# Twelve prepare steps per pair in FFN1, the mixer's running sums in two tiles, head 0's q and k loaded in the last unit

## The chip, the cores and the metric

The kernel runs on one core of a Trainium2 chip. Its time is device microseconds of one execution; the median of several executions is compared. The trace is of one further execution, taken by the hardware profiler. The engines are TensorE (PE, with its weight load PEld), VectorE (DVE), ScalarE (ACT), GpSimd (POOL) and SyncE (SP, which here only issues transfers). All are programmed in order, each with its own queue.

## The reference

One encoder block on x of 1024 tokens by 1024 features, all in float32:

```python
x = layer_norm(a*x + 0.5*swiglu(x, ffn1...))          # FFN1, hidden width 4096
z = x @ w_in                                          # 1024 x 2568: q, k, v, lx, lg, forget logits
fox = forgetting_attention(q, k, v, fg)               # 8 heads of 64, causal, with a forget bias
rec = rg_lru(conv(lx)); lru = gelu(lg) * rec          # a gated linear recurrence, 512 channels
x = layer_norm(a*x + concat(fox, lru) @ w_out)
x = layer_norm(a*x + 0.5*swiglu(x, ffn2...))          # FFN2
```

with a = 2^0.25. `swiglu(x) = (silu(x @ w_gate) * (x @ w_up)) @ w_down`.

## The kernel before

**Numbers and products.** Each float32 operand is split in two parts in a reduced format, `hi` (a cast on ACT) and `lo` (a subtraction on DVE), and a product takes three matmuls (`mm3`, lines 165 to 167). Large products use a seven-product scheme on 2 x 2 blocks (after Strassen and Winograd): the operands are sums and differences of blocks, named "11", "t1", "t2", "s1" and so on, and running sums of products in PSUM give the results.

**FFN1's gate_up.** `gate_up` (line 367 on) goes through 16 pairs of 128-column weight blocks. A pair has two matrices, gate and up. For each matrix, `weights` loads 1 MB (line 400) into one of two "raw" tiles and makes seven operands of two tiles each (`parts`, lines 385 and 386; `less`, line 391) out of the 15 "ws" tiles of a pool. Then come the products, in steps named `one`, (`four` of the matrix before, as `pending`), `two`, `six`, `five`, `seven`, `three`. Some copy the result out of PSUM on ACT (`one` line 690, `six` 696, `five` 700, `four` 709), others add on DVE (`two` 693, `seven` 703, `three` 706). The end of a pair (`finish`, lines 729 to 739) makes the operands of the next stage on DVE and stores them to `h_d` from POOL's queue.

**Prepare steps.** The later stages need kept operands of their weights: those of the mixer's w_in and of the first pair of FFN2. They depend on inputs only, and the generator `prepare` makes them one by one while FFN1 runs. An operand takes a load of 128 KB into one of four "aux" tiles (SP, line 276), sometimes a difference (`less`, line 287), a cast (ACT, line 282) and a subtraction (DVE, line 283) into one "ws" tile of the same pool as the weights, and a store (POOL, line 284) to `wv_d`, `wq_d` or `pre_d`. The generator stops once after its first four loads, and once after each operand: 16 operands for v, 8 units x 2 halves x 7 for the rest of the mixer, 2 matrices x 2 halves x 7 for FFN2, 156 in all. In the loop over pairs 1 to 15, `next(steps)` is called behind three of the six steps of each matrix. What is left afterwards is run in a loop behind `gate_up`:

```python
        for _ in steps:
            pass
```

**FFN1's down_ffn.** It loads the kept operands of `h_d` and blocks of w_down (line 107; the first block goes where operand s3 of gate_up was), splits them (`parts`, lines 810 and 813) and takes seven products.

**The mixer.** `mixer_in` computes z in eight `unit`s of seven products. Units alternate: 128 LRU channels, then 128 columns of q and of k. A unit takes one PSUM tile of two banks, `total` and `z`, from a pool of two (`psS`), and an "a" tile for product "12". In order: "11" into total, copy (1150); "12"; "s2" onto total, copy (1157); "s1" into z, copy (1160); "s3" onto total, add (1163); "s4" onto z, add (1166); "22" onto total. `then[7]` reads total out at the end: LRU units by a copy (line 1201), q/k units by `store`, an activation (1214) and a subtraction (1215) into tiles that go to `q_d` or `k_d` from POOL's queue. Weights come as `wq` (line 1130), three loads ahead. In the last unit the four rows of w_out that belong to the LRU half are loaded (1257) and split (157 and 158).

**Attention.** `attention` takes 64 units (head, block of 128 rows). Scores (1312, 1313), sum with the forget bias and row maximum on DVE (1318), exponential on ACT (1319), scaling on POOL (1322), transposes (1333), values (1354). `load(h)` brings q, k (two parts), cum and v of a head (lines 1291 to 1296). Between units, "pieces" of the output product of the LRU half fill TensorE (`down_tile`, added to the rows of x1 by line 233); `open_row` loads those rows (1396), and `out_w` the other half of w_out (1273).

**What sets the order.** A planner orders the instructions of each engine by the order of the program and by a model of the costs, and inserts the waits. It may move an instruction ahead of its place in the program when it is ready sooner. `issue_after(ins)` forbids what follows on the engine of `ins` to be queued ahead of it; it waits for nothing. Tiles of one tag share the pool's buffers: a tile waits until the last use of the one that had its buffer.

Of the kernel before, what the change touches and what calls it, by code (L numbers as in the profile page):

```python
# [61 lines left out]
class Block:  # L62
# [202 lines left out]
    def prepare(self, jobs, wsp, ap):  # L265
# [104 lines left out]
    def gate_up(self, wg, wu, h_d, rows, bank, tp, wsp, raws=None, later=None, aside=None, ready=None, steps=None):  # L370
# [301 lines left out]
        class Matrix:  # L672
# [22 lines left out]
            def six(m):  # L695
                nc.scalar.copy(m.u, m.product("t2", "s2", m.sum))  # L696

            def five(m):
                m.z = m.product("t1", "s1")
                nc.scalar.copy(m.s5, m.z)  # L700
# [18 lines left out]
        for pair in range(FF // P // 2):  # L719
# [331 lines left out]

    def mixer_in(self, w_out, vw, vp, wp):
# [7 lines left out]
        with self.tc.tile_pool(name="lru_t", bufs=1, reuse_waits="tile") as tp, \  # L1060
# [80 lines left out]
            def unit(c0, c1, c3, then):  # L1141
# [5 lines left out]
                s = self.s_tile()  # L1147
                total, z = s[:, 0, :], s[:, 1, :]
# [9 lines left out]
                done(3)  # L1158
                product(z, "s1")
# [92 lines left out]

            def load_rows():
                for f in range(4):
                    w_rows.append(vp.tile([P, D], F32, tag=f"w{(f + 1) % 4}", name=self.nm("wout")))
                    with self.tc.issue_after(self.row_load.ins):
                        self.row_load = nc.sync.dma_start(w_rows[f], w_out[FOX + f * P:FOX + (f + 1) * P, :])

            def split_row():
                self.lru_w.append(tuple(t[:, 0, :] for t in self.split_ws(w_rows[len(self.lru_w)].rearrange("p (k c) -> p k c", k=1), 1)))  # L1260
# [16 lines left out]
    def attention(self, w_out, mixp, ln, x1_d, normed):  # L1277
# [4 lines left out]
        with self.pool("att_p", 3) as pp, self.pool("att_t", 1) as tp, self.pool("att_pt", 6) as ptp, self.pool("att_qk", 2, side="right") as qkp:  # L1282

            def load(h):
                vt = qkp.tile([P, NT, P], F32R, tag="v", name=self.nm("v"))
                cum = qkp.tile([P, T], F32, tag="cum", name=self.nm("cum"))
                q, kh, kl = (qkp.tile([P, T], F32R, tag=t, name=self.nm(t)) for t in ("q", "kh", "kl"))
                mine = slice(64 * (h % 2), 64 * (h % 2) + 64)
                for j in range(2):
                    rows = slice(64 * j, 64 * j + 64)  # L1290
                    nc.sync.dma_start(f32(q[rows]), self.q_d[h // 2, j, mine, :])
                    nc.sync.dma_start(f32(kh[rows]), self.k_d[h // 2, 0, mine, :])
                    nc.sync.dma_start(f32(kl[rows]), self.k_d[h // 2, 1, mine, :])
                row = self.cum_d[h:h + 1, :]
                nc.sync.dma_start(cum, bass.AP(tensor=row.tensor, offset=row.offset, ap=[[0, P], [1, T]]))
                v_load = nc.sync.dma_start(f32(vt), self.v_d[h].rearrange("(j p) d -> p j d", p=P))
                if h == 0:
                    self.row_load = v_load
                return q, kh, kl, vt, cum
# [106 lines left out]

            piece()
            piece()
# [8 lines left out]
            for n in range(len(units) + AHEAD + 1):  # L1417
# [42 lines left out]
def kernel(  # L1460
# [49 lines left out]
    with blk.psum():  # L1510
        left = ExitStack()
        blk.wsp = left.enter_context(blk.pool("mx_ws", 8))
        with blk.pool("dn_v", side="right") as vp, blk.pool("dn_w", side="right") as wp:
            first = []

            def hooks(norm):
# [6 lines left out]
                def v_weights(g):  # L1523
# [16 lines left out]
                      lambda i: nc.gpsimd.dma_start(x2_d[(i + 4) % NT * P:((i + 4) % NT + 1) * P, :], blk.acc[i]))  # L1540
        rows = blk.acc[4:] + blk.acc[:4]
# [66 lines left out]
```

## Time and profile before

| | |
|---|---|
| runs (us) | 2427.19, 2432.87, 2427.22 |
| median | 2427.22 |
| profiled execution | 2425.57, span 2423.9 |
| TensorE busy | 2290.4 of the span |
| DVE, ACT, POOL busy | 1720.0, 1064.9, 311.1 |
| mean granted clock of TensorE | 0.977 |

The profiled execution is one of its own; its time lies near the median. FFN1's gate_up runs to 641 us, its down_ffn from 726 to about 1030, the mixer's units from 1087 to 1272, attention from 1288 to about 1505, FFN2's gate_up to 2110 and its down_ffn to the end.

In the views quoted below, a wait reads "engine line waited for: total us, times, longest"; a row of the timeline "start, duration, engine, line, operation, output<-inputs", with the idle time before it and what ended it in brackets; a group of instructions "busy us, mean ns of one | idle before and what ended it"; a stretch "from:to, length, busy us (and count) of PE, PEld, DVE, ACT and POOL, granted clock, share of DMA, GB/s"; a transfer "output<-input, queue, count, KB each, us from issue to landing".

### The profile page before, as it was taken

How to read it: one execution, taken by the hardware profiler on the slowest of the kernel's cores; microseconds unless marked ns; L12 is line 12 of the kernel's file. 1: busy time of each engine (PE TensorE's matmuls, PEld its weight loads, DVE VectorE, ACT ScalarE, POOL GpSimd, SP SyncE). 2: the span in 40 equal slices, each digit the busy share in tenths (PEclk: the TensorE clock that was granted, in tenths of full speed). 3: DMA queues.
4: the chain of work that ended last, by engine and by line, in shares of the span. 5: the costliest groups of instructions: out<-in, count | busy, mean ns of one | idle time of the engine just before them, and what ended most of it. 6: DMA issues, size and time to landing. Idle time of an engine off the chain costs nothing.

```text
span 2423.9 us, 29536 instructions
## 1 busy us (share of the span) xinstructions
PE 2290.4 (94%) x10609; PEld 1897.6 (78%) x10609; DVE 1720.0 (71%) x2745; ACT 1064.9 (44%) x1767; POOL 311.1 (13%) x505
## 2 busy tenths in 40 slices
PE   9999999999509999999997999999999999999998
PEld 7888887888408888897776878888888888888887
DVE  8777766676447778786765889766665656567886
ACT  5444443444334434444554675533433333344342
POOL 0132111111350000021112320000000000000000
PEclk9999999999859999999998999999999999999999
DMA  4445454444786643536668673332332323375532
GB/s 148 169 157 176 152 168 148 159 165 159 247 279 244 220 152 135 168 135 206 208 211 241 168 214 132 122 126 83 113 109 87 128 85 113 138 270 178 187 125 85
DMA packets 221202, 394.45 MB, mean 163 GB/s; under 512 B 14256, under 2 KB 123120, under 8 KB 221056
## 3 DMA queue, kind: packets, MB, share of 16 engines
q1 hardware_dynamic: 184352, 268.50, 34.9%
q0 software_dynamic: 36704, 124.07, 13.0%
q8 instruction: 83, 1.36, 0.2%
q14 instruction: 63, 0.52, 0.1%
HBM read 264.56 MB, written 127.96 MB: 162 GB/s over the span
## 4 chain that ended last, share of the span: by engine, by line
PE 63%; DVE 2%; issue 2%; DMA 2%; ACT 2%; SPq 0%; POOL 0%; DVEq 0%; ACTq 0%; POOLq 0%
PE a L166 6%; PE a L167 6%; PE a L165 6%; PE s L165 5%; PE x L167 5%; PE x L165 5%; PE x L166 5%; PE s L167 5%; PE s L166 5%; PE b L167 4%; PE b L166 4%; PE b L165 4%; PE a L1354 1%; DMA kh<-k_d 1%; PE a L1333 1%
## 5 line engine op out<-in xcount | busy, mean ns | idle before, releaser
L385 ACT CAST ws<-t 128x512 fp32r<-128x512 f32 x240 | 148.9, 623 | 359.8 <-PE b L166 140.3
L165 PE MATMUL a<-ws,ws 128*128 128x512 f32 x512 | 200.0, 391 | 85.3 <-ACT ws L810 85.3
L386 DVE TENSOR_TENSOR ws<-t,ws 128x512 fp32r<-128x512 f32 x240 | 164.9, 687 | 87.8 <-PE x L166 38.7
L385 ACT CAST ws<-raw 128x512 fp32r<-128x512 f32 x180 | 111.5, 622 | 234.8 <-PE x L166 134.5
L386 DVE TENSOR_TENSOR ws<-raw,ws 128x512 fp32r<-128x512 f32 x180 | 123.3, 689 | 125.3 <-ACT ws L385 76.7
L165 PE MATMUL b<-As,ws 128*128 128x512 f32 x512 | 200.8, 392 | 4.1 <-ACT row L700 3.6
L166 PE MATMUL a<-ws,ws 128*128 128x512 f32 x512 | 200.1, 391 | 0.7 <-DVE ws L813 0.6
L166 PE MATMUL b<-As,ws 128*128 128x512 f32 x512 | 199.9, 390 | 0.0
L167 PE MATMUL a<-ws,ws 128*128 128x512 f32 x512 | 199.8, 390 | 0.0
L167 PE MATMUL b<-As,ws 128*128 128x512 f32 x512 | 199.7, 390 | 0.0
L165 PE MATMUL x<-As,ws 128*128 128x512 f32 x504 | 196.6, 390 | 0.9 <-ACT row L696 0.9
L166 PE MATMUL x<-As,ws 128*128 128x512 f32 x504 | 196.1, 389 | 0.0
L167 PE MATMUL x<-As,ws 128*128 128x512 f32 x504 | 196.1, 389 | 0.0
L165 PE MATMUL x<-A,ws 128*128 128x512 f32 x496 | 193.5, 390 | 1.7 <-DVE row L703 1.3
L167 PE MATMUL x<-A,ws 128*128 128x512 f32 x496 | 193.0, 389 | 0.0
L166 PE MATMUL x<-A,ws 128*128 128x512 f32 x496 | 193.0, 389 | 0.0
L810 ACT CAST ws<-raw 128x1024 fp32r<-128x1024 f32 x112 | 117.5, 1050 | 163.5 <-PE a L166 83.0
L739 POOL DMA_DIRECT2D h_d<-row x96 | 69.5, 725 | 899.8 <-DVE row L733 830.9
L165 PEld LDWEIGHTS a<-ws,ws 128*128 128x128 f32 x512 | 96.5, 188 | 106.0 <-ACT ws L810 85.7
L813 DVE TENSOR_TENSOR ws<-raw,ws 128x1024 fp32r<-128x1024 f32 x112 | 136.6, 1220 | 51.4 <-ACT ws L810 49.5
L165 PE MATMUL s<-ws,ws 128*128 128x512 f32 x384 | 149.5, 389 | 0.0
L167 PE MATMUL s<-ws,ws 128*128 128x512 f32 x384 | 149.4, 389 | 0.0
(326 smaller groups left out, 5480.3 us busy)
## 6 DMA issues: line engine op xcount, KB each, us to landing
raw<-h_d SPq DMA_DIRECT2D x56, 1024.0 KB, 5.4
h_d<-row POOLq DMA_DIRECT2D x96, 512.0 KB, 3.4
wd<-in_ffn_w_down_dram SPq DMA_DIRECT2D x32, 1024.0 KB, 7.5
raw<-in_ffn_w_gate_dram SPq DMA_DIRECT2D x30, 1024.0 KB, 5.3
raw<-in_ffn_w_up_dram SPq DMA_DIRECT2D x30, 1024.0 KB, 5.3
wq_d<-ws POOLq DMA_DIRECT2D x112, 256.0 KB, 3.6
wq<-wq_d SPq DMA_DIRECT2D x56, 512.0 KB, 3.6
aux<-in_w_in_dram SPq DMA_DIRECT2D x112, 128.0 KB, 3.3
```

Of the source, the lines that this page charges most:

```text
L165: mm(out, ah, bh, start=first, stop=False, skip_group_check=goes_on)
L166: mm(out, ah, bl, start=False, stop=False, skip_group_check=goes_on)
L167: mm(out, al, bh, start=False, stop=last, skip_group_check=goes_on)
L385: nc.scalar.copy(hi, src)
L386: v.tensor_tensor(lo, src, f32(hi), ALU.subtract)
L739: nc.gpsimd.dma_start(d[:, 2 * n:2 * n + 2], t.rearrange("p (r t) -> p r t", r=2))
L810: cast = nc.scalar.copy(hi, src)
L813: self.mark = v.tensor_tensor(lo, src, f32(hi), ALU.subtract)
L1333: nc.tensor.transpose(pa[:, (j % 4) * P:(j % 4 + 1) * P], p[:, j * P:(j + 1) * P], self.ident)
L1354: mm(pv[:, ps], vt[:, j, :], pts[h, qt][j // 4][l][:, j % 4, ps], start=j == 0 and l == 0, stop=j == last and l == 1)
```

## The change

1. In `gate_up`, a place for a prepare step behind each of the six steps of a matrix (`advance`), instead of three. Each step's casts on ACT are now queued behind the last copy out of PSUM (`self.copied`). In `prepare`, one `less` moves to the other side of a stop.
2. In the mixer's `unit`, `total` and `z` get a PSUM tile each.
3. Head 0's q and k are loaded in the last unit behind product "12" (`load_first`), into tiles [128, 2, 1024] that hold two heads side by side and that all heads share. For that the pool `dn_v` stays open through attention. The w_out rows take other tiles and load behind product "s2"; one of them is split inside the unit and three behind it. The pieces and the rows of x1 are redistributed over the first units of attention, and the other half of w_out is loaded behind the last row of x1.

```diff
@@ prepare
-            yield
             a, b = ready[0:2]
             less(a, b)
+            yield
             keep(to["t3"], a)
@@ gate_up
-                nc.scalar.copy(m.s1, m.sum)
+                self.copied = nc.scalar.copy(m.s1, m.sum)
...
+        def advance():
+            if steps:
+                with self.tc.issue_after(self.weight_load.ins), self.tc.issue_after(self.copied.ins):
+                    next(steps, None)
...
                 m.one()
+                advance()
                 if pending:
                     pending()
                 for step in ("two", "six", "five", "seven", "three"):
                     getattr(m, step)()
-                    if steps and step in ("two", "five", "three"):
-                        with self.tc.issue_after(self.weight_load.ins):
-                            next(steps, None)
+                    advance()
@@ mixer_in
+    def load_qk(self, h):
+        nc, b = self.nc, h % 2
+        mine = slice(64 * b, 64 * b + 64)
+        for j in range(2):
+            rows = slice(64 * j, 64 * j + 64)
+            for n, src in (("q", self.q_d[h // 2, j]), ("kh", self.k_d[h // 2, 0]), ("kl", self.k_d[h // 2, 1])):
+                self.row_load = nc.sync.dma_start(f32(self.heads[n][rows, b, :]), src[mine, :])
...
-                s = self.s_tile()
-                total, z = s[:, 0, :], s[:, 1, :]
+                total = self.s_tile()[:, 0, :]
...
+                z = self.s_tile()[:, 0, :]
                 product(z, "s1")
...
+            def load_first():
+                self.heads = {n: vp.tile([P, 2, T], F32R, tag=f"w{k}", name=self.nm(n)) for k, n in enumerate(("q", "kh", "kl"))}
+                self.cum = vp.tile([P, 2, T], F32, tag="w3", name=self.nm("cum"))
+                with self.tc.issue_after(self.row_load.ins):
+                    self.load_qk(0)
...
-                           {3: [self.forget]} if c == 0 else {2: [load_rows], 4: [split_row, split_row], 6: [split_row]} if c == 3 else {})
-            split_row()
+                           {3: [self.forget]} if c == 0 else {2: [load_first], 3: [load_rows], 6: [split_row]} if c == 3 else {})
+            for _ in range(3):
+                split_row()
@@ attention
-            ROWS = {0: 2, 5: 3, 8: 4, 14: 5, 21: 6, 24: 7}
+            ROWS = {0: 2, 4: 3, 11: 4, 14: 5, 21: 6, 28: 7}
+            PIECES = {0: 0, 1: 1, 2: 2}
+            with self.tc.issue_after(self.row_load.ins):
+                heads[0] = load(0)
             open_row(0)
-            heads[0] = load(0)
             open_row(1)
...
-            piece()
-            piece()
...
-                if fill and (n < 1 or n % 8 in (2, 3, 4)):
+                for _ in range(PIECES.get(n, n % 8 in (2, 3, 4)) if fill else 0):
                     with self.tc.issue_after(scores.ins) if n < 3 else nullcontext():
                         piece()
                 if n in ROWS:
                     open_row(ROWS[n])
+                    last_row = self.row_load
                 if 45 <= n < 53 and n % 2:
-                    w_fox.append(next(w_steps))
+                    with self.tc.issue_after(last_row.ins):
+                        w_fox.append(next(w_steps))
```

More of the change, by code (lines that the diff above doesn't have):

```diff
@@ L695, in six @@
             def six(m):
-                nc.scalar.copy(m.u, m.product("t2", "s2", m.sum))
+                self.copied = nc.scalar.copy(m.u, m.product("t2", "s2", m.sum))
             def five(m):
                 m.z = m.product("t1", "s1")
-                nc.scalar.copy(m.s5, m.z)
+                self.copied = nc.scalar.copy(m.s5, m.z)
             def seven(m):
@@ L1281, in attention @@
         lru_tiles = list(zip(self.mix_lru, self.lru_w))
-        with self.pool("att_p", 3) as pp, self.pool("att_t", 1) as tp, self.pool("att_pt", 6) as ptp, self.pool("att_qk", 2, side="right") as qkp:
+        with self.pool("att_p", 3) as pp, self.pool("att_t", 1) as tp, self.pool("att_pt", 6) as ptp, self.pool("att_v", 2, side="right") as vtp:
             def load(h):
[L1285 to L1294, printed above, removed]
+                b = h % 2
+                if h:
+                    with self.tc.issue_after(self.row_load.ins):
+                        self.load_qk(h)
+                row, cum = self.cum_d[h:h + 1, :], self.cum[:, b, :]
                 nc.sync.dma_start(cum, bass.AP(tensor=row.tensor, offset=row.offset, ap=[[0, P], [1, T]]))
[L1296 to L1299, printed above, removed]
+                vt = vtp.tile([P, NT, P], F32R, tag="v", name=self.nm("v"))
+                self.row_load = nc.sync.dma_start(f32(vt), self.v_d[h].rearrange("(j p) d -> p j d", p=P))
+                return *(self.heads[n][:, b, :] for n in ("q", "kh", "kl")), vt, cum
             sums, inv = self.fgz, self.wf.rearrange("p h i -> p (h i)").rearrange("p (h i) -> p h i", h=HEADS)
@@ L1396, in open_row @@
                     self.row_load = nc.sync.dma_start(self.acc[i], x1_d[i * P:(i + 1) * P, :])
-            ROWS = {0: 2, 5: 3, 8: 4, 14: 5, 21: 6, 24: 7}
+            ROWS = {0: 2, 4: 3, 11: 4, 14: 5, 21: 6, 28: 7}
+            PIECES = {0: 0, 1: 1, 2: 2}
+            with self.tc.issue_after(self.row_load.ins):
+                heads[0] = load(0)
             open_row(0)
-            heads[0] = load(0)
             open_row(1)
@@ L1512 @@
         blk.wsp = left.enter_context(blk.pool("mx_ws", 8))
-        with blk.pool("dn_v", side="right") as vp, blk.pool("dn_w", side="right") as wp:
+        high = ExitStack()
+        vp = high.enter_context(blk.pool("dn_v", side="right"))
+        with blk.pool("dn_w", side="right") as wp:
             first = []
@@ L1540 @@
                       lambda i: nc.gpsimd.dma_start(x2_d[(i + 4) % NT * P:((i + 4) % NT + 1) * P, :], blk.acc[i]))
+        high.close()
         rows = blk.acc[4:] + blk.acc[:4]
```

12 lines of the change are left out of this document (7 added, 5 removed).

## The prediction

> **What bounds the kernel now.** I read the engine shares on the page first, then what TensorE waited for, longest first.
>
> ```profile
> span 2423.9 us, 29536 instructions
> PE 2290.4 (94%) x10609; PEld 1897.6 (78%) x10609; DVE 1720.0 (71%) x2745; ACT 1064.9 (44%) x1767; POOL 311.1 (13%) x505
> ...
> PE a L165 <- ACT ws L810: 85.3, 1, 85.3
> PE s L1312 <- DMA kh<-k_d: 14.4, 2, 13.3
> PE s L165 <- ACT raw L1157: 5.4, 8, 0.7
> PE s L165 <- ACT raw L1160: 2.8, 4, 0.7
> ...
> PE a L166 <- DVE w L158: 1.8, 2, 1.1
> ```
>
> TensorE is the bound: 2290 of 2424 us, so 133 us of idle is all that any reordering can recover, apart from time at a lower clock. One wait makes 85.3 us of it, between the last pair of FFN1's gate_up and the first product of its down_ffn. Next come 13.3 us before head 0's scores, and 8.2 us of 0.7 us waits in the mixer. The change touches all three. Busy time by stage (TensorE, weight load, DVE, ACT, POOL, granted clock, DMA share, GB/s) shows what fills them:
>
> ```profile
> 78.00:641.00 563.00, 557.45 (x2443) 458.76 (x2441) 392.39 (x662) 244.47 (x446) 114.58 (x171) 1.00 0.49 163
> 641.00:726.30 85.30, 0.01 (x1) 0.00 (x1) 37.93 (x91) 23.88 (x60) 40.33 (x58) 0.52 0.87 294
> 726.30:731.00 4.70, 4.61 (x13) 3.27 (x14) 4.61 (x5) 2.33 (x3) 0.00 (x0) 0.64 0.15 17
> 1080.00:1262.00 182.00, 172.67 (x766) 136.96 (x765) 124.17 (x221) 92.02 (x141) 26.73 (x43) 1.00 0.63 216
> 1535.00:2098.00 563.00, 563.00 (x2485) 466.33 (x2485) 351.70 (x518) 216.80 (x352) 40.79 (x60) 1.00 0.30 104
> ```
>
> The first and last rows are the two gate_up stages, FFN1's with prepare steps inside and FFN2's without any. The second row is the gap. What runs in it:
>
> ```profile
> L283 DVE TENSOR_TENSOR ws<-aux,ws 128x256 fp32r<-128x256 f32 x57 | 23.1, 424 | 28.2 <-ACT ws L282 28.2
> ...
> L283 DVE TENSOR_TENSOR ws<-aux,ws 128x256 fp32r<-128x256 f32 x156 | 63.1, 422 | 71.4 <-ACT ws L282 71.2
> L287 DVE TENSOR_TENSOR aux<-aux,aux 128x256 f32<-128x256 f32 x80 | 33.6, 424 | 28.8 <-DMA aux<-in_w_in_dram 20.6 <-DMA aux<-in_ffn_w_gate_dram 3.9 <-DMA aux<-in_ffn_w_up_dram 3.0
> ```
>
> 57 of the 156 kept operands are made after gate_up, while TensorE stands. DVE and ACT are less than half busy there: it is a chain of load, cast, subtract and store, not a full engine.
>
> **Part 1: six places per matrix.** The generator has 157 stops (one for the first loads, 156 operands). The loop has 15 pairs of 2 matrices: 90 places before, 180 after. So 157 / 12 = 13.1 pairs use all of them up, and the drain loop behind gate_up finds nothing. The 85.3 us do not go to zero, because the next load is late then. FFN1's first block of w_down comes late for its own reason, in the loads' queue:
>
> ```profile
> 636.29 0.42 SPq L107 DMA_DIRECT2D wd<-in_ffn_w_down_dram  x1
> ...
> wd<-in_ffn_w_down_dram SPq DMA_DIRECT2D x2, 1024.0 KB, 7.0
> ...
> 726.30 1.28 PE L165 MATMUL a<-ws,ws 128*128 128x512 f32 x2 [85.29 <-ACT ws L810]
> ...
> 2111.07 0.50 PE L166 MATMUL a<-ws,ws 128*128 128x512 f32 x1 [0.59 <-DVE ws L813]
> ...
> L810 ACT CAST ws<-wd 128x1024 fp32r<-128x1024 f32 x1 | 1.0, 1045 | 0.9 <-ACT ws L810 0.9
> ```
>
> TensorE stopped at 726.3 - 85.3 = 641.0; the block was issued 4.7 us earlier, when the memory of operand s3 came free, and takes 7.0 us. It lands 2.3 us after the stop; with the cast of 1.0 us and some 1.2 us for the first remainders (FFN2's own start waits 0.6) about 4.5 us of idle stay. Gain 85.3 - 4.5 = 81. The clock costs the same twice: after the gap 13 matmuls took 4.7 us, where FFN2's rate (563 us / 2485 = 0.227) gives 2.9, so 1.8 us are lost at the half clock, and a shorter gap loses them again:
>
> ```profile
> 399.33 0.62 ACT L385 CAST ws<-t 128x512 fp32r<-128x512 f32 x1 [3.99 <-DMA wq_d<-ws]
> 402.06 0.79 PE L165 MATMUL b<-As,ws 128*128 128x512 f32 x1 [2.19 <-ACT row L700]
> 402.65 0.63 PE L166 MATMUL b<-As,ws 128*128 128x512 f32 x1
> ```
>
> Here a wait of 2.19 us was enough for matmuls of 0.63 us instead of 0.39. [...]
>
> The same rows show what the moved steps can cost. Steps and weights share 15 "ws" tiles, taken in turn. When the planner put several step casts close together, ACT's weight cast waited 3.99 us for a step's store to land, the copy of s5 behind it on ACT was late, and TensorE stood 2.19 us. FFN1's gate_up lost 563 - 557.45 = 5.5 us in this way, plus some 2 us of clock. Each pair now takes 28 + 12 = 40 tiles instead of 34, so a tile comes round after 15/40 of a pair (168 x 0.227 = 38.1 us), 14.3 us instead of 16.8. Against that, each step's cast now sits behind a copy out of PSUM, so no six of them can run in one bunch. Throughput is there: steps cost DVE 63.1 + 33.6 = 97 us; over 13.1 pairs (499 us) that adds 0.19 to FFN2's 351.7 / 563 = 0.62, so 0.81. DMA goes from 0.30 by 0.19 x (157/99) x (563/499) to about 0.64; twice the loads on SP and stores on POOL (rows of both with rival 5) leave both queues mostly free. The order of `less` before the stop moves 0.42 us of DVE and nothing else. The step loads stand behind the pair's weight load on SP as before. I take +2 us, from -7 (all stalls gone) to +20 (below).
>
> **Part 2: two tiles for the running sums.** No instruction is added. The 0.7 us waits are on a copy out of the other half of the same tile: L1157 copies from `total` and the product held up writes `z`. With a tile each the order of reads and writes asks for nothing here, so 5.4 + 2.8 = 8.2 us go. What is late next: both tiles now belong to one unit, and the next unit's "11" can no longer be slipped into this one. It needs a free tile: z's, read out by L1166 during "22" and so free in time, or, if tiles are taken strictly in turn, total's:
>
> ```profile
> 1223.90 0.39 PE L167 MATMUL s<-xT,wq 128*128 128x512 f32 x1
> 1227.81 0.69 DVE L1215 SCALAR_TENSOR_TENSOR ev<-s,ev 128x512 fp32r<-128x512 f32 x1 [5.20 <-DMA k_d<-ev]
> ...
> 1246.12 0.39 PE L167 MATMUL s<-xT,wq 128*128 128x512 f32 x1
> 1246.99 0.57 ACT L1201 COPY zx<-s 128x512 f32<-128x512 f32 x1
> ```
>
> These are the last reads of a total after its unit's end: up to 4.2 us late (1228.5 - 1224.3) in a q/k unit, 1.1 us (1247.6 - 1246.5) in an LRU unit. In turn, that is at most 4 x 1.1 + 3 x 4.2 = 17 us, less what "12", which needs neither tile, covers. I take -8, from -8 to +9.
>
> **Part 3: head 0.** TensorE had 13.3 us of idle because its loads started when the mixer was over, behind a prefetch of w_out:
>
> ```profile
> 1270.01 1.77 SPq L1273 DMA_DIRECT2D raw<-in_w_out_dram  x2
> 1271.89 0.80 SPq L1291 DMA_DIRECT2D q<-q_d  x1
> ...
> 1288.06 1.19 PE L1312 MATMUL s<-kh,q 128*128 128x512 f32 x2 [13.27 <-DMA kh<-k_d]
> ...
> 1256.00:1260.00 4.00, 3.28 (x15) 2.41 (x14) 2.22 (x4) 4.00 (x7) 0.00 (x0) 1.00 1.01 344
> ...
> 1276.00:1280.00 4.00, 0.00 (x0) 0.00 (x0) 1.88 (x3) 0.00 (x0) 0.54 (x1) 0.50 1.00 409
> ...
> q<-q_d SPq DMA_DIRECT2D x16, 256.0 KB, 6.4
> ```
>
> After the change the six loads go out behind product "12" of the last unit, four products (4 x 2.7 = 11 us) and the gates before its end, and w_out's two 1 MB blocks stand behind the last x1 row. At 6.4 us each and one queue, q and k are there when the unit ends. The four w_out rows, which feed the fill pieces, wait for "s2" and follow in the queue with cum: 1.5 + 2 + 0.5 MB behind 1 MB of wq at the 344 to 409 GB/s of the two rows is 12 to 15 us, about the unit's end. So scores start at once, but the piece tied behind scores(1) and the first reduction can wait: scores(1) takes a PSUM tile whose last reader, L1215, came 5 us after the unit here too (1276.89). The wait of 13.3 us and its slow clock (matmuls run at clock 0.5, about 2 us) and 1.8 us on late w_out splits make 17; I keep about 4 as left, so -13, from -17 to -3.
>
> [...]
>
> **The rest.** Sharing a tile between two heads adds no wait between its halves: in the old kernel rows 0 and 1 of x1 share one, and the sums on row 0 ran at 1277.5 before row 1's load left at 1283. The moved x1 rows and pieces keep their number; this stage idled 6 us of 160. I take 0, +-3.
>
> ```profile
> 1277.50 1.27 DVE L233 SCALAR_TENSOR_TENSOR row<-row,a 128x512 f32<-128x512 f32 x2
> 1283.11 2.65 SPq L1396 DMA_DIRECT2D row<-x_d  x2
> ...
> 1300.00:1460.00 160.00, 154.11 (x969) 133.03 (x968) 131.64 (x327) 111.95 (x261) 50.55 (x106) 1.00 0.65 184
> ```
>
> **Sum.** -81 + 2 - 8 - 13 + 0 = -100 us. The profiled execution took 2425.6 us (span 2423.9), 1.6 below the median of 2427.2; on the median that is 2327 us.
>
> **Rivals.**
> 1. The steps starve the weights. If each of 13 pairs has one stall as at 402 us (2.2 us and 1.8 us of clock), that is 52 us instead of 7: 2327 - 2 + 45 = 2370. For: more tiles per pair, DVE at 0.81. Against: spread casts, and 99 steps ran inside with only 5.5 us lost.
> 2. Tiles are taken in turn. Part 2 becomes +9: 2344.
> 3. Head 0's loads only move the wait to cum, x1 row 0 and the w_out rows, which now share memory with x1's rows. Part 3 is -3: 2337.
> 4. The steps still end behind gate_up, since the planner may issue later than written. Then only parts 2 and 3 count: 2406. Against: it already pulled about ten (99 against 89) ahead of their places.
> 5. Slower than before: step stores queue on POOL behind h_d stores that wait for DVE:
>
> ```profile
> POOL h_d L739 <- DVE row L733: 231.5, 13, 21.4
> ...
> wq_d<-ws POOLq DMA_DIRECT2D x112, 256.0 KB, 3.6
> ...
> L284 POOL DMA_DIRECT2D wq_d<-ws x112 | 77.6, 726 | 185.5 <-DVE ws L283 182.5 <-DVE aux L287 2.6 <-issue 0.2
> ```
>
> If one holds a "ws" tile for 21.4 + 0.7 + 3.6 (the store's landing) = 25.7 us against the 14.3 us in which the tile is wanted again, each of 13 pairs stalls 11.4 us: 148 us, so 2327 + 146 = 2473. It decides from 100 / 13 = 7.7 us per pair. Against: such waits stand on POOL now, and the longest wait for a tile is 4 us.
>
> **How the numbers follow.** My forecast 0.60, rival 1 0.12, rival 2 0.13, rival 3 0.09, rival 4 0.02, rival 5 0.04. The likeliest case alone spans about 2315 to 2340. For 8 in 10 I go down to 2310 (all waits of parts 2 and 3 and the stalls gone) and up to 2353, which holds rivals 2 and 3 and the mild half of rival 1. All but rival 5 are faster by over 0.3% (7 us), the least that a measurement tells from none: faster 0.96. Of rival 5's 0.04 I give 0.01 to a stall that just balances the gain.
>
> **What would show it.** Right: no wait of 85 us on L810 but one of 2 to 6; no L282 casts after gate_up; the waits on L1157 and L1160 gone; the first scores within 2 us of the last unit. Wrong: waits on wq_d stores that grow in FFN1's gate_up, waits on L1201 or L1215 copies at unit starts, or a new wait on w_out rows or cum.

## The result and the profile after

The changed kernel takes 2333.4 us (median of four runs, 2331.2 to 2335.1) against 2427.2 of the kernel before in the same comparison: ratio 0.961, 95% interval 0.959 to 0.963. The profiled execution took 2331.2 us. Of the changed kernel, the span, the engines' busy time and the longest waits of TensorE (line numbers from here on are those of the changed kernel where it is the one shown; lines behind the edits moved by up to some 17):

```profile
span 2329.2 us, 29518 instructions
PE 2290.3 (98%) x10609; PEld 1896.2 (81%) x10609; DVE 1704.9 (73%) x2745; ACT 1063.3 (46%) x1767; POOL 310.3 (13%) x505
...
PE x L167 <- DVE ws L386: 4.7, 9, 1.0
PE x L165 <- ACT row L696: 4.7, 2, 3.5
PE s L1329 <- DVE ev L1228: 3.1, 1, 3.1
PE s L1329 <- DVE raw L1179: 3.0, 1, 3.0
PE a L165 <- ACT ua L974: 2.2, 5, 0.5
PE a L166 <- DVE ue L975: 2.0, 5, 0.8
```

TensorE's busy time did not change (2290.3 and 2290.4 us). The 85.3 us wait, the 13.3 us wait on head 0's k and the waits on copies inside the mixer's units are gone. No single wait of over 4 us is left, but there are new ones, on the engines that prepare data.

From the first product of a stage to the first of the next, in the two traces:

| stretch | before | after | difference |
|---|---|---|---|
| FFN1's gate_up, with the gap behind it | 713.7 | 639.7 | -74.0 |
| FFN1's down_ffn, and v | 360.8 | 360.2 | -0.6 |
| the eight units, up to the first scores | 200.9 | 171.5 | -29.4 |
| first scores to the first transposes | 11.1 | 22.0 | +10.9 |
| the rest, to the end | 1124.7 | 1125.3 | +0.6 |

The second and third row from below belong together, because scores(0) now run ahead of the last unit's product "22" and the rest of the scores wait. Together they are -18.5 us. The first product itself starts 2.0 us earlier, but this start lies anywhere between 10.6 and 13.5 us in the traces of the experiments below, so it is not put down to the change. The gap, first the loads on SyncE's queue before and after, then TensorE's start of down_ffn after:

```profile
621.80 14.40 SPq L276 DMA_DIRECT2D aux<-in_w_in_dram  x10
636.29 0.42 SPq L107 DMA_DIRECT2D wd<-in_ffn_w_down_dram  x1
```
```profile
642.29 0.37 SPq L107 DMA_DIRECT2D wd<-in_ffn_w_down_dram  x1
...
650.25 0.39 PE L165 MATMUL a<-ws,ws 128*128 128x512 f32 x1
651.09 0.96 PE L165 MATMUL a<-ws,ws 128*128 128x512 f32 x3 [0.45 <-ACT row L709]
```

After the change the first block of w_down is issued 650.25 - 642.29 = 8.0 us before TensorE needs it, not 4.7, and TensorE waits 0.45 us. In SyncE's queue after, this load waited for TensorE alone, for a product of the last pair:

```profile
SPq L107 <- PE b L167: 31.6, 1, 31.6
```

Before, ten operand loads of prepare steps stood ahead of it in SyncE's queue until 636.2, and of a wait for TensorE behind them the trace shows 0.3 us at most.

What was lost instead lies inside gate_up. A pair without a stall takes 38.1 us in both kernels. The 15 pairs behind the first lose 10.0 us against that before and 20.6 after. All of the 20.6 lies in the pairs with steps; the last two pairs, which have none left, take 38.1.

### The profile page after: what moved, and what is told of

It reads as the page before. It is cut to its first block, busy times and chain, and to the rows that moved or that the text cites. A ratio compares the mean times of both kernels' runs of the same rounds, so it can differ in the third digit from the quotient of the medians.

```text
span 2329.2 us, 29518 instructions
## 1 busy us (share of the span) xinstructions
PE 2290.3 (98%) x10609; PEld 1896.2 (81%) x10609; DVE 1704.9 (73%) x2745; ACT 1063.3 (46%) x1767; POOL 310.3 (13%) x505
## 4 chain that ended last, share of the span: by engine, by line
PE 72%; issue 7%; DVE 3%; ACT 2%; DMA 2%; POOL 1%; DVEq 0%; POOLq 0%; ACTq 0%; SPq 0%
PE x L167 6%; PE x L165 6%; PE x L166 6%; PE a L166 6%; PE a L167 6%; PE a L165 6%; PE b L165 5%; PE b L166 5%; PE b L167 5%; PE s L166 5%; PE s L167 5%; PE s L165 5%; PE a L1371 1%; PE a L1350 1%; POOL wq_d L284 1%
## 5 line engine op out<-in xcount | busy, mean ns | idle before, releaser
L385 ACT CAST ws<-t 128x512 fp32r<-128x512 f32 x240 | 147.7, 622 | 311.7 <-PE b L166 139.4
L386 DVE TENSOR_TENSOR ws<-t,ws 128x512 fp32r<-128x512 f32 x240 | 164.2, 686 | 59.5 <-ACT ws L385 35.5
L385 ACT CAST ws<-raw 128x512 fp32r<-128x512 f32 x180 | 110.4, 621 | 172.5 <-PE x L166 136.2
L386 DVE TENSOR_TENSOR ws<-raw,ws 128x512 fp32r<-128x512 f32 x180 | 123.1, 687 | 85.2 <-ACT ws L385 74.3
L165 PE MATMUL s<-ws,ws 128*128 128x512 f32 x384 | 149.5, 389 | 0.0
L167 PE MATMUL s<-ws,ws 128*128 128x512 f32 x384 | 149.4, 389 | 0.0
L166 PE MATMUL s<-ws,ws 128*128 128x512 f32 x384 | 149.4, 389 | 0.0
```

The source lines that it names most:

```text
L165: mm(out, ah, bh, start=first, stop=False, skip_group_check=goes_on)
L166: mm(out, ah, bl, start=False, stop=False, skip_group_check=goes_on)
L167: mm(out, al, bh, start=False, stop=last, skip_group_check=goes_on)
L385: nc.scalar.copy(hi, src)
L386: v.tensor_tensor(lo, src, f32(hi), ALU.subtract)
```

## The experiments

Every kernel was compared with the kernel before on the same chip. The whole-kernel intervals are about 4 us to either side, so where a difference is smaller, the stretch in the trace is compared, and the text says so. There is one trace of each kernel, and such a stretch scatters too: with the same gate_up it was 710.1 to 714.2 us in three kernels, and 638.9 to 641.9 in four.

### Each part alone

Part 1: the diff's hunks in `prepare` and `gate_up`. Part 2: `total` and `z` in tiles of their own. Part 3: all the hunks on head 0 and attention.

> The kernel before with the new places for the step calls alone (six per matrix, each behind the copy before it). If the three parts add up (theory): the change's own stretch from the first gate_up product to down_ffn, -74 us, is all from these places, so about 2353 us, with 0.4 us of gap left ahead of down_ffn and pairs of gate_up some 10 us longer in sum than their 38.1 us. Rival: part of the 74 us comes with the other two edits (they shift the streams ahead): then the stretch gains under 70 us and the time is above 2357.

> The kernel before with the two sums of a mixer unit in a PSUM tile of their own each, alone. If the units' gain is what the waits before showed (theory): the four units lose their boundary waits, -8 to -9 us there, and the mixer's end keeps its wait on head 0's loads as it was: about 2418.5 us. Rival 1: the freed time only makes head 0's loads wait longer, since they end on SP's queue: about 2427. Rival 2: three tiles in turn make total wait: 2427 or more.

> The kernel before with head 0's q and k loaded inside the last unit, and the new order at the start of attention, alone; the two sums of a unit still share one PSUM tile, so only one of the three tiles is taken by the last unit and scores(0) finds a free one. Theory A (in the kernel after it is the tile that z still holds that keeps scores(0) and scores(1) waiting): without it the scores start within 1 us of the last unit, about -15 us, so 2412. Rival B (VectorE is late there whatever tile is asked for, its splits are what the start waits for): -9 to -10 us, what parts two and three brought together less the units' own 8.8, so 2418.

Measured: part 1 alone 2356.0 us (ratio 0.970, 0.967 to 0.972), part 2 alone 2409.9 (0.992, 0.991 to 0.994), part 3 alone 2413.0 (0.994, 0.992 to 0.996). Of the three, TensorE's rows on head 0 and the units:

```profile
PE s L1316 <- DMA kh<-k_d: 17.3, 3, 16.1
PE s L165 <- ACT raw L1161: 5.4, 8, 0.7
```
```profile
PE s L1312 <- DMA kh<-k_d: 9.2, 2, 7.8
```
```profile
PE s L165 <- ACT raw L1166: 5.4, 8, 0.7
PE s L1325 <- DVE ev L1224: 5.1, 1, 5.1
```

- The spans differ from the span before by 67.4, 14.2 and 11.2 us, in sum 92.8; the full change's span differs by 94.7. That nearness is in part chance: the medians of the runs differ by 72.7, 18.7 and 15.6 us, in sum 107 where the full change gives 94. **Part 1 stands by itself, parts 2 and 3 overlap.** Of part 1's 67.4, 71.8 are won in gate_up's stretch (74.0 in the full change), so the rival falls; 2.2 are given back where head 0's k is waited for (16.1 us, not 13.3), and 2.9 behind the first transposes. From the first unit to the first transposes part 2 alone gains 16.0 us and part 3 alone 10.8, together only 18.5.
- **Part 2 alone gained more than the waits it removed.** They were 8.2 us; the stretch from the first unit to the first scores became 15.9 us shorter (200.9 to 185.1). The wait on k fell from 13.3 to 7.8 us as well: in this kernel two pieces of the output product (24 matmuls, 5.4 us) run behind the last unit, while the loads are under way, where before only 5 matmuls did. Neither rival came true.
- **Part 3 alone** starts the scores before the last unit ends, but scores(1) then wait 5.1 us for VectorE's last read of the unit's total. Its 10.8 us from the first unit to the first transposes are rival B's size: without the second PSUM tile the same wait is there. Theory A falls. The ratio alone (-11 to -19 us) would not have told, since gate_up happened to run 3.6 us faster in the profiled execution.

### Where gate_up loses its 20 us: the order of the casts

In the trace after, all twelve casts of a pair lie close together, about 19 to 35 us into it, and the casts of the next pair's weights begin only behind them (before, with six, at about 26 us). Of the kernel after, ACT's timeline in one pair (it starts at about 221 us):

```profile
239.91 0.41 ACT L282 CAST ws<-aux 128x256 fp32r<-128x256 f32 x1
240.23 0.58 ACT L690 COPY row<-x 128x512 f32<-128x512 f32 x1
242.45 0.41 ACT L282 CAST ws<-aux 128x256 fp32r<-128x256 f32 x1 [1.65 <-issue]
...
244.34 1.19 ACT L282 CAST ws<-aux 128x256 fp32r<-128x256 f32 x3
247.04 0.41 ACT L282 CAST ws<-aux 128x256 fp32r<-128x256 f32 x1 [1.51 <-DVE aux L287]
249.69 0.41 ACT L282 CAST ws<-aux 128x256 fp32r<-128x256 f32 x1 [2.24 <-DMA aux<-in_w_in_dram]
```

My first theory was the bunch itself. Splitting it:

```diff
-            for m, view in zip((gate, up), self.gu_views(wg, wu)):
-                weights(pair, view, m.w)
+            views = self.gu_views(wg, wu)
+            if steps is None or pair == 1:
+                weights(pair, views[0], gate.w)
+            else:
+                gate.w.update(ahead)
+            weights(pair, views[1], up.w)
             for m in (gate, up):
+                if steps and m is up and pair < FF // P // 2 - 1:
+                    ahead = {}
+                    weights(pair + 1, views[0], ahead)
```

> The kernel after, with the weights of the next pair's gate matrix converted between the products of gate and up, and not with those of up at the head of the pair: the steps' casts of a pair then fall in two bunches of six and not in one of twelve. Theory (the 10 us that gate_up's pairs gained come from the bunch of twelve steps ahead of the next weights): -8 to -10 us if the steps then spread, at least half of it; 2323 to 2328 us, gap ahead of down_ffn still under 1 us. Rival (the time is lost to the steps' load on VectorE and ScalarE as such, or to the rings behind them): the losses only move to the other matrix, 2333 us.

Measured: 2331.6 us (2330.2 to 2334.2), gate_up's stretch 640.2 us: no gain. The bunches did split, six casts at 0 to 10 us of a pair and six at 20 to 30. TensorE's waits in gate_up (60 to 660 us), first after, then with the bunch split:

```profile
PE x L167 <- DVE ws L386: 4.7, 9, 1.0
PE x L165 <- ACT row L696: 4.7, 2, 3.5
PE x L165 <- ACT ws L385: 1.2, 3, 0.7
...
PE b L165 <- ACT row L700: 0.2, 1, 0.2
```
```profile
PE x L165 <- ACT row L696: 7.3, 8, 2.5
PE b L165 <- ACT row L700: 5.5, 10, 1.4
```

The waits for weights (L385, L386) are gone, and the waits for copies out of PSUM (L696, L700) rose from 4.9 to 12.8 us. TensorE waits for whatever the casts happen to stand ahead of. A smaller bunch did not help: the theory fell, and the rival's time held.

Two more edits of the order. One left out the steps in the pair that alone lost 7.0 us after the change (`if steps and pair != 3`); the other dropped the order behind the copies.

```diff
-                with self.tc.issue_after(self.weight_load.ins), self.tc.issue_after(self.copied.ins):
+                with self.tc.issue_after(self.weight_load.ins):
```

> The kernel after without step calls in the fourth pair of gate_up (the one in which the mixer's constants are loaded and converted); the steps go on one pair later, and the last pair but one gets those that are left. Theory (the 7.0 us that this pair lost come from casts of steps that meet the constants' work on ScalarE and VectorE): this pair falls back to about 39 us, -5.8 us, 2327.5 us in all, since the same number of casts costs about 1 us in the pair that takes them instead. Rival (the constants' work alone holds up the copy): the pair stays at 45 us, 2333 us.

> The kernel after with the same six places per matrix, but each step call no longer held behind the copy ahead of it. Theory from the run with the gate's weights moved (there the weight waits went to nothing and the waits on the copies rose from 4.9 to 12.8 us: PE waits wherever casts stand ahead of what it needs next): the casts may now come ahead of copies, the waits on the copies grow, +3 to +10 us, 2336 to 2343. Rival (the casts are held by the loads of their operands, so the order behind the copies never binds): the same bunch of twelve, 2333 us.

Measured: without steps in that pair 2330.4 us (2328.4 to 2335.1). The pair fell from 45.1 to 38.9 us as the theory said, but the stretch of gate_up is 639.5, the same: other pairs took over, one going from 39.5 to 42.8 and one from 40.6 to 42.3. So the expectation of about 1 us in the pair that takes them failed, and the rival that the constants alone held up the copy failed too. Without the order behind the copies 2335.9 us (2331.8 to 2337.4), gate_up's stretch 645.1, +5.4; the waits on L690, L696 and L700 came to 7.0 us, against 5.2 after, and those on L386 to 7.5 against 4.7. The order behind copies seems to help by a few us, at the low end of the theory (the times alone do not tell the two kernels apart), and it does not spread the casts: the bunch is still there without it.

### Where gate_up loses its 20 us: the loads

ACT's rows above show another thing: 244.3 to 249.7 us is mostly idle between casts, which wait for a difference on VectorE or for a load. The view of line 276, the operand loads, over nine pairs (213 to 560 us), before (the same stretch is about nine pairs there too) and after:

```profile
  DVE aux L287: 6.0, 10
  ACT ws L282: 1.3, 1
```
```profile
  DVE aux L287: 21.7, 17
  ACT ws L282: 11.7, 11
...
DMA to landing us min/median/max: 2.1/3.2/5.5
```

With twice the steps the two engines wait 33.4 us for operands and not 7.3. There are four operand tiles; a step's load is issued when an earlier step gives its tile back, and takes 3.2 us. SyncE's longest wait with these loads, after, over the same nine pairs, shows the first part:

```profile
SPq L276 <- DVE aux L287: 88.8, 46, 5.9
```

What stands behind the waiting instruction comes late too, weights and copies. In the pair with the 3.5 us wait on L696, after, a cast on L282 at 169.06 us had waited 2.43 us for its difference, the copy behind it on ACT began at 169.67, and TensorE stood 3.45 us for that copy. With the bunch split, the two engines' waits for operands came to 10.8 + 2.4 = 13.2 us, and yet TensorE lost as much. There another ring is waited for, that of the 15 "ws" tiles, where the next tile can be one whose step's store has not landed yet. Over the nine pairs, with the bunch split:

```profile
ACT ws L385 <- DMA wq_d<-ws: 21.5, 15, 2.3
ACT ws L282 <- DMA wq_d<-ws: 10.1, 8, 2.3
```
```profile
DVE ws L386 <- DMA wq_d<-ws: 13.1, 12, 2.1
```

In the kernel after, ACT waited 9.0 + 1.8 us in these two rows and VectorE not at all. So the split took waits from one ring and gave them to the other; that these are what TensorE then lost by is likely, and no run shows it. Two kernels tell this from the order. The first leaves work out (its text says what); the second moves the differences.

```diff
-                t = ap.tile([P, 2 * P], F32, tag="aux", name=self.nm("aux"))
-                t = t.rearrange("p (k f) -> p k f", f=src.shape[-1])
-                nc.sync.dma_start(t, src)
-                ready.append(t)
+                if len(first) < 4:
+                    t = ap.tile([P, 2 * P], F32, tag="aux", name=self.nm("aux"))
+                    first.append(t)
+                    nc.sync.dma_start(t.rearrange("p (k f) -> p k f", f=src.shape[-1]), src)
+                t = first[count[0] % 4]
...
-            v.tensor_tensor(x, x, y, ALU.subtract)
+            v.tensor_tensor(x, x, y, ALU.min)
```
```diff
-            v.tensor_tensor(x, x, y, ALU.subtract)
+            nc.gpsimd.tensor_tensor(x, x, y, ALU.subtract)
```

> The kernel after without the loads of the steps' operands: the first four blocks are loaded once and used over and over, with a minimum in place of the subtraction so that the values stay bounded. It leaves out 260-odd loads of 128 KB and computes the mixer's weights wrongly; the casts, subtractions and stores of the steps all stay. Theory (the twelve casts of a pair take 15 us for 5 us of work on each engine since they wait for operands in a ring of four, L287 21.7 us and L282 11.7 us over nine pairs, and what stands behind them on VectorE and ScalarE is late by that): the bunch gets shorter, the 20 us that the pairs of gate_up lose fall to 10 us or less, about 2323 us. Rival (it is the order alone, twelve casts and subtractions between two engines that hand each to the other, not the loads): 16 to 20 us stay, 2329 to 2333 us.

> The kernel after with the differences of the steps (four in six steps, 0.42 us each on VectorE) on GpSimd. VectorE's queue then no longer stands behind the loads of operands (21.7 us over nine pairs) nor spends 5 per cent of its time on them. Theory (VectorE's share is what the products wait for, L386 4.7 us): that wait falls under 2 us and the pairs lose 12 to 15 us and not 20, about 2327 us. Rival (ScalarE's casts wait for the differences all the same and hand the delay on, or GpSimd is slower at them and its stores of h_d come later): 20 us or more, 2333 to 2340 us.

Measured: without the loads 2311.2 us (ratio 0.9525, 0.951 to 0.954). (The trace after has 136 loads on line 276 for the 156 operands, so the number of loads in the expectation was too high.) TensorE's waits in gate_up and down_ffn's start of this kernel (60 to 690 us), all of them:

```profile
PE a L165 <- ACT row L712: 0.5, 1, 0.5
PE b L165 <- ACT row L703: 0.2, 1, 0.2
```

The 15 pairs lose 1.0 us in all, and gate_up's stretch is 619.2 us, 20.5 less than after. All casts, subtractions and stores of the steps are still there, in bunches of twelve, and they cost nothing. **The loss in gate_up hangs on the steps' loads.** The rival, the order between two engines alone, is out. What it is about the loads is not separated: without them this stage also moves less data (DMA share 0.47 and not 0.58), and ACT's waits for wq_d stores fell with them, from 10.8 to 2.9 us.

With the differences on GpSimd 2364.3 us (ratio 0.974, 0.973 to 0.976), 31 slower than after; gate_up's stretch is 676.7. Of this kernel, GpSimd's row for the differences (60 to 600 us) and ACT's longest wait in total (213 to 560 us):

```profile
L287 POOL TENSOR_TENSOR aux<-aux,aux 128x256 f32<-128x256 f32 x76 | 66.0, 922 | 26.3 <-DMA aux<-in_w_in_dram 20.9 <-DMA aux<-in_ffn_w_gate_dram 3.9 <-issue 1.2
```
```profile
ACT ws L282 <- POOL aux L287: 72.2, 45, 3.6
```

VectorE was freed, but the same loads held GpSimd, whose difference takes 922 ns where VectorE's takes 424, and ACT's casts waited 72.2 us for them (33.5 after). That is the rival, and larger than either expectation. The waits for line 276 themselves came to 20.1 + 7.2 = 27.3 us, no more than after, so what this run adds is likely the slower difference. Load, difference, cast and subtraction are one chain, and moving a link to another engine did not shorten it.

### The start of attention

scores(0) waited 3.0 us and scores(1) 3.1 us. Of the kernel after, VectorE at that place:

```profile
1181.19 0.68 DVE L1179 TENSOR_TENSOR raw<-s,raw 128x512 f32<-128x512 f32 x1
1184.50 0.69 DVE L1228 SCALAR_TENSOR_TENSOR ev<-raw,ev 128x512 fp32r<-128x512 f32 x1 [2.62 <-ACT w L157]
1185.11 4.80 DVE L158 TENSOR_TENSOR w<-wout,w 128x1024 fp32r<-128x1024 f32 x4
1189.84 0.68 DVE L1228 SCALAR_TENSOR_TENSOR ev<-s,ev 128x512 fp32r<-128x512 f32 x1
1190.44 1.21 DVE L1335 CUSTOM_DVE_ANT_0 p<-s,cum 128x1024 f32<-128x1024 f32 x1
```

L1179 is the last read of the unit's `z`, and scores(0) start at 1181.93, when it is done. L1228 from s is the last read of `total`. It stands behind four splits of w_out's rows, and the first reduction (L1335) stands behind it. Two edits, one for the tile and one for the queue:

```diff
-                z = self.s_tile()[:, 0, :]
+                z = self.a_tile() if z_in_a else self.s_tile()[:, 0, :]    # z_in_a: the last unit
```
```diff
-            for _ in range(3):
-                split_row()
+            with self.tc.issue_after(self.last_store.ins):    # L1228 from s
+                [split_row() for _ in range(3)]
```

> The kernel after, with the second running sum of the very last mixer unit in one of the half tiles and not in a tile of the scores' kind, so that scores(0) and scores(1) each find a tile that nobody reads any more. Theory (the starts of scores(0) and scores(1) waited 3.0 and 3.1 us for those tiles and ran at half clock behind that): the two waits go, at most 6 us and the half clock behind them are won; since the first reductions still stand behind the four 1.2 us splits on VectorE I expect 3 to 5 us, 2328 to 2330 us. Rival (the splits set the time of the first transposes whatever the tiles): the wait only stands at the first transposes or pieces, 2333 us.

> The kernel after with both edits, no step calls in the fourth pair and the last second sum in a half tile: they lie in stages that share nothing, so the two gains add up, -9 to -11 us, 2322 to 2325 us. If either rival holds, only the other's gain is seen.

> The kernel after with the last three splits of W_out's rows ordered behind the last read of the unit's first sum; in the order of VectorE that read now comes behind one split and not behind four. Theory (what keeps scores(1) and the first transposes waiting is that read, queued behind 4.8 us of splits): the 3.1 us wait of scores(1) goes and the first transposes come 3 to 5 us sooner, 2328.5 to 2330.5 us. Rival (the pieces of W_out that fill TensorE behind scores(1) need all four splits, so that TensorE waits for these in turn): the wait moves to the pieces, and the first transposes come at the same time, 2333 us.

Measured: with z in a half tile 2330.3 us (2329.3 to 2331.9), with the skipped pair as well 2330.9 (2329.7 to 2332.5). From the first unit to the first transposes these take 191.4 and 191.5 us, five other kernels that leave this place as it is 191.4 to 192.4, the kernel after 193.5: no gain that can be told. The scores start some 6 us sooner, but "22" of the last unit then waits for its weights (3.3 us, 2.2 in the other) and scores(1) again for L1228 (2.6 and 5.1 us): the rival.

With the late splits 2329.9 us (2326.9 to 2334.5; ratio 0.9605, 0.959 to 0.962, which alone does not tell it from the kernel after). The place itself shows a gain: 189.5 us from the first unit to the first transposes, and 190.1 in the last kernel below, which has the same edit, 1.2 to 4 us below the eight just named. scores(1) wait 1.4 us and not 3.1, so the splits made 1.7 us of that wait. The theory's place was right, its size (3 to 5 us) too large; the gain is seen in two traces and not in the times.

### A version with six operand tiles

The last kernel does the whole work: six operand tiles, the bunch split in two of six, the late splits. The memory for two more tiles was taken from the ring that weights and steps share.

```diff
-            blk.pool("gu_ws", 15) as wsp, blk.pool("aux", 4) as ap, ...
+            blk.pool("gu_ws", 14) as wsp, blk.pool("aux", 6) as ap, ...
```

> A version that does the whole work: the kernel after with six operand tiles for the steps and not four (their two more KB per partition come from the ring of operands, 14 tiles and not 15), the gate's weights converted between the products of gate and up as in the run above, so that a bunch has six steps and needs six operands, and the late splits. Theory (the loads of the steps' operands in a ring of four hold VectorE and ScalarE, and that is all that gate_up's pairs lose: without these loads they lost 1 us in 15 pairs): all six operands of a bunch are there when it begins, the waits on L276 fall under 4 us over nine pairs and the pairs lose under 6 us and not 21; with 3 us from the splits about 2314 us (2310 to 2319). Rival (with 14 tiles the casts of the weights wait longer for TensorE and the loss only moves to L385): 10 us or more stay, 2322 to 2330 us.

Measured: 2322.3 us (2319.6 to 2322.6), ratio 0.9565 (0.9545 to 0.9585): some 11 us below the changed kernel and 104 below the kernel before, the fastest that does the whole work. gate_up's stretch is 632.9 us and its 15 pairs lose 14.0 us, not 20.6 and not under 6. Over nine pairs, who waited for line 276 in this kernel, and two of ACT's waits:

```profile
  DVE aux L287: 20.5, 16
```
```profile
ACT ws L385 <- DMA wq_d<-ws: 18.1, 19, 2.8
...
ACT ws L282 <- DMA wq_d<-ws: 16.8, 13, 2.9
```

The theory fell: the waits for operands did not go under 4 us, nor the loss under 6. The rival's numbers held (10 us or more, 2322 to 2330), but not its reason. ACT's waits for a "ws" tile whose store has not landed are 18.1 + 16.8 = 34.9 us here against 10.8 after, but with 15 tiles and the bunch split they were already 21.5 + 10.1 = 31.6. So they come with the order of the casts, and the shorter ring added little. That kernel, with the bunch split, is also the fair one to compare with in gate_up, since only the two rings differ there: the stretch fell by 7.3 us (640.2 to 632.9), while the waits for operands rose from 13.2 to 20.5 and VectorE's waits for wq_d stores fell from 13.1 to 3.0. Six operand tiles thus did not remove the waits for operands, and what won the 7.3 us stays open. Six operand tiles with 15 "ws" tiles were not tried.

## Why the prediction was right, and where it was not

**The time.** 2327 was forecast, 2333.4 measured, inside the likeliest case's own range (2315 to 2340). The profiled execution took 94.4 us less, where the sum said 100. That it came so near is partly luck: the gap came out 4 us better than forecast for a reason that the forecast had wrong, and gate_up's pairs 8.6 us worse.

**The gap, -81.** Its size is right and the reason for the rest is not. The 85.3 us went to 0.45, not to 4.5. The step that failed is "issued 4.7 us earlier, when the memory of operand s3 came free". In the trace before, ten operand loads stood ahead of that load in SyncE's queue, so it was late for the very reason the change removes. It now goes out 8.0 us ahead. TensorE's wait is 4 us shorter than forecast.

**gate_up's stalls, +2.** This is the term that missed: 20.6 - 10.0 = 10.6 us more, inside the range given for it (-7 to +20). Three steps of its argument are involved. "Each step's cast now sits behind a copy out of PSUM, so no six of them can run in one bunch" is wrong: twelve ran in one bunch, and taking that order away changed the stretch by 5 us and not the bunch. "Twice the loads on SP and stores on POOL ... leave both queues mostly free" was the wrong place to look. What binds is the steps' loads, 3.2 us each into four tiles in turn: the run without these loads (-20.5 us) shows it for the loads, while the part of the four tiles in it is argued. I had priced the "ws" ring, which the stores hold, and never the "aux" ring. The waits for wq_d stores even fell: over the nine pairs ACT and VectorE waited 32.8 us for them before, 10.8 after. The row of L287 in the prediction (28.8 us of idle time, most of it on loads) already showed VectorE waiting for operands; that row and the one above it, with 156 subtractions, are of the whole program, though they stand there as a part of the gap, where L287 idled 17.8 us. The shares were no warning. The 13 pairs with steps, after:

```profile
59.00:574.00 515.00, 503.80 (x2184) 409.62 (x2183) 388.91 (x716) 245.96 (x474) 151.71 (x224) 0.99 0.63 213
```

VectorE is busy for 389 / 515 = 0.76 (0.81 forecast) and DMA 0.63 (0.64): neither is the limit.

**Part 2, -8.** The waits named are gone (L1157 and L1160, now L1169 and L1173, do not appear among TensorE's waits), and no wait at a unit's start took their place. Instead the gates wait 4.2 us in ten small pieces for the convolution (L974 and L975), which the forecast did not have. Part 2 alone shortened the span by 14 us, more than its waits, since pieces of the output product then ran during the loads' wait; that part of the gain is time that part 3 takes away too, so in the full change it counts once. Together the two parts were forecast at -21 and gave -18.5.

**Part 3, -13.** "Scores start at once" failed: scores(0) waited 3.0 us for `z`, and "scores(1) takes a PSUM tile whose last reader, L1215, came 5 us after the unit here too" was the right worry at the right place (3.1 us). The 4 us kept for it were nearly enough. What I missed is why that reader is late. Before, it waited for a store:

```profile
1276.89 0.69 DVE L1215 SCALAR_TENSOR_TENSOR ev<-s,ev 128x512 fp32r<-128x512 f32 x1 [3.35 <-DMA k_d<-ev]
```

After, four splits stand ahead of it on VectorE. The change has three of them behind the unit where the program had one.

**The rivals.** 1, starved weights, is the one that came true in part: not 45 us but 8.6 more than forecast, and by the operands' loads, not the ring of the weights' tiles. 2 did not: no wait on a total at a unit's start. 3 did not in its form: no wait on cum, x1 or the w_out rows' loads. 4 did not: the last of L282's casts runs at 593 us, and gate_up ends at 650. 5 did not: the longest wait in the pairs with steps is 3.5 us, and ACT and VectorE waited less for the steps' stores than before.

## What to carry to other kernels

When background work is made denser, price each ring of buffers that it goes through, the small one of its inputs first: uses per bunch against tiles, and the landing time of a load (3.2 us here) against the time in which the bunch needs the next. In these runs an instruction that waited for its operand held up what stood behind it on its engine (after: 2.43 us for a cast ahead of a copy, 3.45 us for TensorE behind that copy), so the wait showed up in TensorE's list under other lines (weights in one kernel, 4.7 us on L386; copies in another, 12.8 us). A new order can move waits from one ring to another at the same loss, as splitting the bunch did (operands 33.4 to 13.2 us, ACT's waits for wq_d stores 10.8 to 31.6). To find the cause, take away what the background work waits for, and see whether the main work still stalls. And compare each version with the one that differs from it in one thing only.

## What the runs showed of the hardware

The length of TensorE's wait does not alone decide whether the clock falls behind it. In the kernel before, a wait of 2.19 us at 402 us was followed by 3.4 us at half clock. Behind a longer one, 2.47 us at 111 us in the kernel with the split bunch, the clock did not fall: it was 1.00 over the 5 us around this wait.

```profile
111.21 0.50 PE L165 MATMUL x<-As,ws 128*128 128x512 f32 x1 [2.47 <-ACT row L696]
```

Columns as in the prediction, first two stretches of the kernel before, then one of the split bunch:

```profile
399.00:406.00 7.00, 4.81 (x15) 3.51 (x14) 5.01 (x8) 2.76 (x5) 0.00 (x0) 0.76 0.01 5
401.96:405.38 3.42, 3.32 (x8) 2.65 (x9) 2.78 (x5) 1.08 (x3) 0.00 (x0) 0.50 0.00 0
```
```profile
107.00:112.00 5.00, 2.53 (x11) 1.80 (x10) 4.20 (x7) 1.95 (x4) 2.03 (x3) 1.00 1.02 405
```

What else decides it, these two waits do not show.

Beside that, one difference of 128 x 256 float32 numbers took 922 ns on GpSimd and 424 ns on VectorE.
